# Score products of a head pair as two 64-row products into two banks, and value products of the two halves placed side by side

## The chip, the cores and the metric

The kernel runs on one core of one Trainium2 chip. The metric is the device time of one execution in microseconds (us), as the median of three runs. A core has a matmul engine (TensorE: PE for the products, PEld for the loads of the stationary operand), VectorE (DVE), ScalarE (ACT), GpSimd (POOL) and SyncE (SP), whose queue issues nearly all loads here. Matmul results land in PSUM, which has eight banks of 512 fp32 columns over 128 partitions.

## The reference

Two layers over 256 tokens of width 1024. Layer 0 mixes with a differential attention (4 heads, two score maps each) and an indexed sparse attention (8 query heads on 2 key heads; an indexer of 4 heads of 64 picks 64 keys per query), then a dense feed-forward block. Layer 1 mixes with a block attention (8 heads) and a three-branch attention (8 query heads on 2 key heads: compressed, selected and window keys), then a mixture of 8 experts, of which each token takes 2. With 256 tokens the selected and the window branch and the block attention are all plain causal attention. All heads are 64 wide.

```python
def diff_attention(q, k, v, lam_params, subln_w, lam_init):
    ...
        s = jnp.einsum('bqhjd,bshjd->bhjqs', qb, k, preferred_element_type=F32) * scale
        ...
        p = masked_softmax(s, mask)
        w = p[:, :, 0] - lam * p[:, :, 1]
        return jnp.einsum('bhqs,bshe->bqhe', w.astype(v.dtype), v)
...
def dsa_attention(q, k, v, iq, ik, iw):
    ...
        logits = jnp.einsum('bqhd,bsd->bqhs', iqc, ik, preferred_element_type=F32)
        score = jnp.einsum('bqh,bqhs->bqs', iwc.astype(F32), jax.nn.relu(logits))
        ...
        s = jnp.einsum('bqgrd,bqkgd->bgrqk', qc, kg, preferred_element_type=F32) * scale
        p = masked_softmax(s, ok[:, None, None]).astype(dt)
        return jnp.einsum('bgrqk,bqkgd->bqgrd', p, vg)
...
for l in range(DEPTH):
    x = layer_norm(alpha * x + mixer(x))
    x = layer_norm(alpha * x + (swiglu(x) if l == 0 else moe_swiglu(x)))
```

The last four lines are shortened from the reference's main loop.

## The kernel before, in words

All 256 tokens are two tiles of 128 (NT = 2, index t for rows, qt for queries). Weights are read from HBM as raw tiles of 128x1024 fp32 (load_raw, L115, issued on SP's queue in program order), split into a rounded part wh (ScalarE, L142) and a rest wl (VectorE, L144), and multiplied in three products per block (mm3, L152). The number of raw tiles is fixed; a load waits in SP's queue until the tile that it overwrites has been read. The order of the instructions on each engine is planned by the framework from a simulated timeline, so a function's work may be mixed with that of others; on each engine the planned order is then fixed, and an instruction that waits holds up those behind it. Allocation order in a pool decides which buffer a tile gets.

The attention part works on pairs of heads. Queries are held transposed, 128 partitions for a pair: rows 0 to 63 are one head, 64 to 127 the other (to_heads, L321: transposes into one bank, one copy out). Keys are held the same way but in blocks (to_blocks, L328; blocks_tile, L337): for a pair there are two copies of the width, in the first of which rows 64 to 127 are zero, in the second rows 0 to 63. The zeros are written once by GpSimd (L339, L340), and to_blocks copies the two halves of rows out of PSUM with one instruction each. One product of 128 rows with a moving operand of 2 x nk columns then gives the scores of both heads side by side in one bank.

softmax8 (L346) does this for the eight heads of one query tile with nk = 128 keys (qt = 0) or 256 keys (qt = 1). It goes through groups that fill one bank: two pairs of heads (qt = 0) or one pair (qt = 1). For each group it takes a bank "sps", writes the mask into it with a bf16 product (L356), adds the score products (L359), takes the row maxima with one VectorE instruction (L361) and makes the exponentials on ScalarE, one instruction per head (L364). The banks "sps" come from a ring of two (tag "sp", shared with "hps" of to_heads and a few others). It is called five times for each query tile: diff_probs (keys akB), dsa_probs (bkB), twice in nsa_start (ksB, kwB) and in moba (ckB). The indexer (L455 to L464) makes its scores in the same manner with ikB, two products per query tile, and one Relu per bank (L464).

pv_T (L373) makes the value products transposed: for each key block and each half (first or second head of the pairs) it transposes four blocks of probabilities into a bank "ptps" (L379), copies them out (evac, which alternates between ScalarE and VectorE), and multiplies: with shared values (L385) one product of 512 columns whose result has 64 rows; otherwise (moba, L388) four products of 128 columns. The two halves write the rows 0 to 63 and 64 to 127 of one bank oT.

After the attention come the output projection (mixer_out, L272), a layer norm and, in layer 1, the router and then the experts (L1231), whose weights come in 672 loads of 512 KB.

Of the kernel before, what the change touches and what calls it, by code (L numbers as in the profile page):

```python
# [8 lines left out]
F32 = mybir.dt.float32  # L9
# [4 lines left out]
AF = mybir.ActivationFunctionType  # L14
# [3 lines left out]
P = 128  # L18
# [21 lines left out]
def hybrid_kernel(ctx, tc, x, ev_w_in, ev_w_out, dif_lambda, dif_subln, ffd_w_gate, ffd_w_up, ffd_w_down,  # L40
# [287 lines left out]
    def to_blocks(dst, srcs, t):  # L328

        ps = bank((P, 4, P), "hps")  # L330
        for i, s in enumerate(srcs):
            nc.tensor.transpose(ps[:, i], s, ident)
        for half in range(2):
            r = slice(half * 64, half * 64 + 64)
            evac(dst[r, :, half, t * P:(t + 1) * P], ps[r, :len(srcs)])

    def blocks_tile(pool, n, name):  # L337
        b = pool.tile([P, n, 2, S], F32, name=name)
        nc.gpsimd.memset(b[0:64, :, 1], 0.0)  # L339
        nc.gpsimd.memset(b[64:128, :, 0], 0.0)  # L340
        return b
# [4 lines left out]
    def softmax8(pool, qT, kb_, kslot, qt, maskb, sums):  # L346


        nk = (qt + 1) * P
        ns = 512 // (2 * nk)  # L350
        nm = pool.tile([P, 8], F32, tag="nm", name="nm", bufs=3)
        e = [pool.tile([P, 4, S], F32, tag="e", name="e", bufs=NE_) for _ in range(2)]
        mk = maskb.shape[-1]
        for s0 in range(0, 4, ns):
            ps = bank((P, 2 * ns, nk), "sps")
            nc.tensor.matmul(ps[:, :, nk - mk:], identb, maskb[:, None, :].to_broadcast([P, 2 * ns, mk]),  # L356
                             start=True, stop=False, skip_group_check=True)
            for j in range(ns):
                nc.tensor.matmul(ps[:, 2 * j:2 * j + 2], qT[:, s0 + j, qt * P:(qt + 1) * P],  # L359
                                 kb_[:, kslot(s0 + j), :, :nk], start=False, stop=j == ns - 1, skip_group_check=True)  # L360
            nc.vector.tensor_reduce(nm[:, 2 * s0:2 * (s0 + ns)], ps, axis=AX.X, op=ALU.max, negate=True)  # L361
            for j in range(2 * ns):
                i = 2 * s0 + j
                nc.scalar.activation(e[i // 4][:, i % 4, :nk], ps[:, j], AF.Exp, bias=nm[:, i:i + 1],  # L364
                                     accum_out=sums[:, i:i + 1])
        return e
# [6 lines left out]
    def pv_T(pool, oT, e, qt, vsl, shared, first=True, last=True):  # L373

        for kb in range(qt + 1):
            for half in range(2):
                ps = bank((P, 4, P), "ptps")
                for s_ in range(4):
                    nc.tensor.transpose(ps[:, s_], e[s_ // 2][:, s_ % 2 * 2 + half, kb * P:(kb + 1) * P], ident)  # L379
                pT = pool.tile([P, 4, P], F32, tag="pT", name="pT", bufs=3)  # L380
                evac(pT, ps)
                o = oT[half * 64:half * 64 + 64]
                end = last and kb == qt
                if shared:
                    nc.tensor.matmul(o, vsl(half, kb), pT, start=first and kb == 0, stop=end, skip_group_check=True)  # L385
                else:
                    for s_ in range(4):
                        nc.tensor.matmul(o[:, s_], vsl(2 * s_ + half, kb), pT[:, s_],  # L388
                                         start=first and kb == 0 and s_ == 0, stop=end, skip_group_check=True)
# [29 lines left out]
    bkB = blocks_tile(ap, 1, "bkB")  # L419
    bv = ap.tile([P, NT, P], F32, name="bv")  # L420
    iqT = ap.tile([P, 2, S], F32, name="iqT")
    ikB = blocks_tile(ap, 1, "ikB")
# [3 lines left out]
    akB = blocks_tile(ap, 4, "akB")  # L426
# [3 lines left out]
    def c_b(t, ps):  # L430
        r = roped()
        rope(ap, ps[:, 0:128], 2, t, r[:, 0:128])
        rope(ap, ps[:, 256:512], 4, t, r[:, 256:512])
        nc.scalar.copy(bv[:, t], ps[:, 128:256])
        to_blocks(bkB, [r[:, 0:128]], t)
        to_heads(iqT, [r[:, 256:384], r[:, 384:512]], t)

    def c_i(t, ps):
        r = roped()
        rope(ap, ps[:, 0:64], 1, t, r[:, 0:64])  # L440
        nc.vector.tensor_copy(r[:, 64:128], r[:, 0:64])
        nc.vector.tensor_copy(iw[:, t], ps[:, 64:68])
        to_blocks(ikB, [r[:, 0:128]], t)
# [11 lines left out]
    for qt in range(NT):  # L455
        nk = (qt + 1) * P
        rl = ap.tile([P, 4, S], F32, tag="e", name="rl", bufs=NE_)
        ns = 512 // (2 * nk)
        for s0 in range(0, 2, ns):
            ps = bank((P, 2 * ns, nk), "ips")  # L460
            for j in range(ns):
                nc.tensor.matmul(ps[:, 2 * j:2 * j + 2], iqT[:, s0 + j, qt * P:(qt + 1) * P], ikB[:, 0, :, :nk],
                                 start=True, stop=True)
            nc.scalar.activation(rl[:, 2 * s0:2 * (s0 + ns), :nk], ps, AF.Relu)  # L464
        sc = ap.tile([P, S], F32, tag="score", name="score", bufs=2)
        nc.vector.tensor_scalar(sc[:, :nk], rl[:, 0, :nk], iw[:, qt, 0:1], None, op0=ALU.mult)
        for h in range(1, 4):
            nc.vector.scalar_tensor_tensor(sc[:, :nk], rl[:, h, :nk], iw[:, qt, h:h + 1], sc[:, :nk],
                                           op0=ALU.mult, op1=ALU.add)
        nc.vector.tensor_tensor(sc[:, nk - P:nk], sc[:, nk - P:nk], causalb, ALU.add)  # L470
        m8 = ap.tile([P, 8], F32, tag="m8", name="m8", bufs=2)
        for _ in range(TOPK // 8):
            nc.vector.max(m8, sc[:, :nk])
            nc.vector.match_replace(sc[:, :nk], m8, sc[:, :nk], GONE)
        sb = ap.tile([P, nk], BF16, name=f"selb{qt}")
        nc.vector.tensor_scalar(sb, sc[:, :nk], -2e38, NEG, op0=ALU.is_gt, op1=ALU.mult)
        nc.vector.tensor_tensor(sb[:, nk - P:], sb[:, nk - P:], causalb, ALU.min)
        selb[qt] = sb

    def dsa_probs(qt):  # L480
        return weighted(ap, bqT, bkB, lambda s: 0, qt, selb[qt])
# [6 lines left out]
    def diff_probs(qt):  # L488
        nk = (qt + 1) * P
        sums = ap.tile([P, 8], F32, tag="sums", name="sums", bufs=3)  # L490
        e = softmax8(ap, aqT, akB, lambda s: s, qt, causalb, sums)
# [40 lines left out]
    project(xp, w0[:, 512:1024], 512, c_rope(to_blocks, akB, False))  # L532
# [97 lines left out]
    ksB = blocks_tile(ap, 1, "ksB")  # L630
    kwB = blocks_tile(ap, 1, "kwB")
# [3 lines left out]
    ckB = blocks_tile(lp, 4, "ckB")  # L635
# [17 lines left out]
    def c_kv(t, ps):  # L653
        nc.scalar.copy(kvc[:, t], ps[:, 0:256])
        nc.scalar.copy(vsw[:, t, 0], ps[:, 384:512])
        r = roped()
        rope(ap, ps[:, 256:384], 2, t, r[:, 0:128])
        to_blocks(ksB, [r[:, 0:128]], t)

    def c_w(t, ps):  # L660
# [3 lines left out]
        to_blocks(kwB, [r[:, 0:128]], t)  # L664
# [135 lines left out]
    def nsa_start(qt):  # L800
        oT = mbank("oT", "mo").rearrange("p (s q) -> p s q", q=P)
        for i, kb_ in ((0, ksB), (1, kwB)):
# [16 lines left out]
    def moba(qt):  # L819
        e = weighted(lp, cqT, ckB, lambda s: s, qt, causalb)  # L820
# [84 lines left out]
    project(xp, w1[:, 512:1024], 512, c_rope(to_blocks, ckB, False))  # L905
# [388 lines left out]
```

## Time and profile before

| | us |
|---|---|
| median of 3 runs | 1399.73 (1396.94 to 1402.06) |
| profiled execution | 1404.08 |
| its span, first to last instruction | 1402.2 |
| TensorE busy in the span | 1313.6 (94%) |
| VectorE busy | 753.4 (54%) |
| ScalarE busy | 544.3 (39%) |
| mean granted TensorE clock | 0.967 |

The span has two parts. Up to about 520 us the DMA engines are busy for parts of the time; from there to the end they are busy throughout, at some 400 GB/s. Layer 0's attention lies between about 20 and 122 us, its feed-forward block up to about 310, layer 1's projections and attention between about 310 and 490, the router up to 520.

How to read the rows further below. A row of the stretches has the stretch, its length, then the busy time of PE, PEld, DVE, ACT and POOL (instructions in brackets), the granted clock as a share of 2.4 GHz, the DMA engines' busy share and GB/s. A row of the timeline has the start, the length, the engine, the line and the operation with what it writes and reads, the tile of the array (contraction rows * output rows), the moving operand's shape and how many instructions were merged into the row; in square brackets how long the engine was idle before and what ended it. An fp32 product stands there as two instructions. The length of a matmul includes its way through the array; in a stream the next one starts earlier. A row of a tile or line has the count, then the shortest, median and longest duration in ns, the first and last start, and the shapes.

### The profile page before, as it was taken

To read this page: it belongs to the slowest core of one execution; us is meant where nothing else is said; L and a number is where in the kernel's file an instruction comes from. 1 tells how busy PE (TensorE), PEld (TensorE's weight loads), DVE (VectorE), ACT (ScalarE), POOL (GpSimd) and SP (SyncE) were. 2 spreads that over 40 slices of the span, in tenths; PEclk is the share of its full clock that TensorE was granted. 3 is DMA by queue.
4 is the path that set the end of the run, shared out by engine and by line. 5 is a ranking of instruction groups with operands and counts; after the bars stand their busy time and mean duration, and the time that the engine had idled before them with its cause. 6 is when DMAs were issued, how large, how long until landed. Compare 5 with 4: busy or idle time off the path is not lost. (4 is left out here: it accounts for less than half of the span.)

```text
span 1402.2 us, 18209 instructions
## 1 busy us (share of the span) xinstructions
PE 1313.6 (94%) x6136; PEld 848.1 (60%) x6136; DVE 753.4 (54%) x1194; ACT 544.3 (39%) x796; POOL 48.9 (3%) x79
## 2 busy tenths in 40 slices
PE   8979999998988989999999999999999999999983
PEld 7856888886864753367873356885446886433221
DVE  5977654548577551178863156794227894301004
ACT  4464453533436311066652055673125673100000
POOL 2200000001220000000000000000000000000000
PEclk9999999999999979999999998999999999999996
DMA  9244645535453459999999999998999999999993
GB/s 352 70 135 145 216 162 198 184 118 191 148 151 120 156 200 404 402 409 409 402 397 398 402 409 409 402 383 343 408 402 409 408 402 377 409 402 409 409 402 114
DMA packets 146805, 429.98 MB, mean 307 GB/s; under 512 B 15696, under 2 KB 23280, under 8 KB 146704
## 3 DMA queue, kind: packets, MB, share of 16 engines
q1 hardware_dynamic: 146000, 426.48, 80.2%
q0 software_dynamic: 704, 2.26, 0.5%
q8 instruction: 50, 0.82, 0.2%
q14 instruction: 51, 0.42, 0.1%
HBM read 427.64 MB, written 1.05 MB: 306 GB/s over the span
## 5 line engine op out<-in xcount | busy, mean ns | idle before, releaser
L144 DVE TENSOR_TENSOR wl<-raw,wh 128x1024 fp32r<-128x1024 f32 x378 | 455.3, 1224 | 120.3 <-ACT wh L142 117.2
L142 ACT CAST wh<-raw 128x1024 fp32r<-128x1024 f32 x378 | 389.5, 1047 | 230.0 <-PE pg L158 58.4
L1115 PE MATMUL pgu<-raw,xs 128*64 128x512 f32 x1120 | 266.0, 607 | 3.9 <-DMA raw<-in_moe_w_up_dram 3.1
L1115 PEld LDWEIGHTS pgu<-raw,xs 128*64 128x64 f32 x1120 | 81.6, 139 | 164.5 <-issue 132.2
L1160 PE MATMUL y<-raw,hT_s 128*64 128x512 f32 x560 | 130.8, 598 | 7.2 <-DMA raw<-in_moe_w_down_dram 5.5
L1123 DVE TENSOR_TENSOR h_s<-h_s,pgu 64x512 f32<-64x512 f32 x35 | 24.1, 689 | 190.0 <-ACT h_s L1122 190.0
L1160 PEld LDWEIGHTS y<-raw,hT_s 128*64 128x64 f32 x560 | 37.5, 136 | 93.9 <-issue 62.3
L1122 ACT ACTIVATE h_s<-pgu 64x512 f32<-64x512 f32 x35 | 20.7, 591 | 180.2 <-PE pgu L1115 180.2
L156 PE MATMUL mmps<-wh,xTh 128*128 128x512 f32 (+2 forms) x192 | 76.5, 399 | 1.2 <-ACT wh L142 1.0
L158 PE MATMUL mmps<-wh,xTl 128*128 128x512 f32 (+2 forms) x192 | 75.6, 395 | 1.8 <-DVE xTl L165 1.7
L157 PE MATMUL mmps<-wl,xTh 128*128 128x512 f32 (+2 forms) x192 | 74.3, 389 | 0.5 <-DVE wl L144 0.5
L157 PE MATMUL pg<-wl,xeh 128*128 128x512 f32 x168 | 71.1, 423 | 3.8 <-DVE wl L144 3.8
L156 PE MATMUL pg<-wh,xeh 128*128 128x512 f32 x168 | 72.0, 429 | 1.7 <-ACT wh L142 1.3
L158 PE MATMUL pg<-wh,xel 128*128 128x512 f32 x168 | 70.3, 418 | 0.0
L157 PE MATMUL y<-wl,hTh 128*128 128x512 f32 x168 | 66.7, 397 | 1.2 <-DVE wl L144 1.0
L156 PE MATMUL y<-wh,hTh 128*128 128x512 f32 x168 | 66.6, 396 | 0.8 <-ACT wh L142 0.8
L158 PE MATMUL pu<-wh,xel 128*128 128x512 f32 x168 | 66.8, 397 | 0.0
L157 PE MATMUL pu<-wl,xeh 128*128 128x512 f32 x168 | 66.6, 397 | 0.0
L158 PE MATMUL y<-wh,hTl 128*128 128x512 f32 x168 | 66.2, 394 | 0.0
L156 PE MATMUL pu<-wh,xeh 128*128 128x512 f32 x168 | 65.4, 389 | 0.0
L317 ACT COPY hT_s<-tps 128x256 f32<-128x256 f32 x18 | 6.7, 372 | 135.9 <-PE tps L1142 135.9
L319 DVE COPY hT_s<-tps 128x256 f32<-128x256 f32 x17 | 7.2, 425 | 96.9 <-PE tps L1142 96.9
(376 smaller groups left out, 1918.6 us busy)
## 6 DMA issues: line engine op xcount, KB each, us to landing
raw<-in_moe_w_up_dram SPq DMA_DIRECT2D x224, 512.0 KB, 10.1
raw<-in_moe_w_gate_dram SPq DMA_DIRECT2D x224, 512.0 KB, 10.1
raw<-in_moe_w_down_dram SPq DMA_DIRECT2D x224, 512.0 KB, 10.1
raw<-in_ffd_w_gate_dram SPq DMA_DIRECT2D x22, 512.0 KB, 5.1
raw<-in_ffd_w_up_dram SPq DMA_DIRECT2D x22, 512.0 KB, 4.5
raw<-in_ffd_w_down_dram SPq DMA_DIRECT2D x22, 512.0 KB, 4.7
raw<-in_ev_w_in_dram SPq DMA_DIRECT2D x20, 512.0 KB, 9.0
raw<-in_od_w_in_dram SPq DMA_DIRECT2D x20, 512.0 KB, 4.1
```

The costliest lines, as they stand in the source:

```text
L142: nc.scalar.copy(wh[:, :w], rv)
L144: nc.vector.tensor_tensor(wl[:, :w], rv, wh[:, :w].bitcast(F32), ALU.subtract)
L156: nc.tensor.matmul(ps, ah, wh, start=first and i == 0, stop=False)
L157: nc.tensor.matmul(ps, ah, wl, start=False, stop=False)
L158: nc.tensor.matmul(ps, al, wh, start=False, stop=last and i == n - 1)
L317: nc.scalar.copy(dst, src)
L319: nc.vector.tensor_copy(dst, src)
L1115: nc.tensor.matmul(p_[i * SMALL:(i + 1) * SMALL], xs[:, k0 + k], halves(w[k], n)[j], start=k0 + k == 0, stop=k0 + k == KD - 1)
L1122: nc.scalar.activation(h[:SMALL], p_[:SMALL], AF.Silu)
L1123: nc.vector.tensor_tensor(h[:SMALL], h[:SMALL], p_[SMALL:], ALU.mult)
L1160: nc.tensor.matmul(ys[0][i * SMALL:(i + 1) * SMALL], ts[k], w[:, i * 512:(i + 1) * 512], start=c0 == 0 and k == 0, stop=c0 + n == F_EXP an ...
```

## The change

The keys lose their blocks of zeros: a tile of keys is half as wide, is filled by to_heads as the queries are, and nothing is set to zero. Each score product of a pair becomes two products of 64 contraction rows, one from rows 0 to 63 of queries and keys into one bank, the other from rows 64 to 127 into a second bank. A group of softmax8 now covers two banks at once: all four pairs (qt = 0) or two pairs (qt = 1), with one mask product and one maximum per bank, so the number of mask products, maxima and exponentials stays as it was; the exponentials alternate between the two banks. The indexer does the same, with one Relu per bank written to every second head. In pv_T both halves are transposed and copied out first, and then their products follow each other: the two halves of the shared product, or, in moba, the halves in turn for each of the four pairs.

```diff
-    def to_blocks(dst, srcs, t):
-        ps = bank((P, 4, P), "hps")
-        for i, s in enumerate(srcs):
-            nc.tensor.transpose(ps[:, i], s, ident)
-        for half in range(2):
-            r = slice(half * 64, half * 64 + 64)
-            evac(dst[r, :, half, t * P:(t + 1) * P], ps[r, :len(srcs)])
-
-    def blocks_tile(pool, n, name):
-        b = pool.tile([P, n, 2, S], F32, name=name)
-        nc.gpsimd.memset(b[0:64, :, 1], 0.0)
-        nc.gpsimd.memset(b[64:128, :, 0], 0.0)
-        return b
+    def keys_tile(pool, n, name):
+        return pool.tile([P, n, S], F32, name=name)
+
+    HALVES = (slice(0, 64), slice(64, P))
...
         nk = (qt + 1) * P
-        ns = 512 // (2 * nk)
+        ns = 512 // nk
         nm = pool.tile([P, 8], F32, tag="nm", name="nm", bufs=3)
+        nv = nm.rearrange("p (s h) -> p h s", h=2)
...
         for s0 in range(0, 4, ns):
-            ps = bank((P, 2 * ns, nk), "sps")
-            nc.tensor.matmul(ps[:, :, nk - mk:], identb, maskb[:, None, :].to_broadcast([P, 2 * ns, mk]),
-                             start=True, stop=False, skip_group_check=True)
+            pss = [bank((P, ns, nk), "sps") for _ in HALVES]
+            for ps in pss:
+                nc.tensor.matmul(ps[:, :, nk - mk:], identb, maskb[:, None, :].to_broadcast([P, ns, mk]),
+                                 start=True, stop=False, skip_group_check=True)
             for j in range(ns):
-                nc.tensor.matmul(ps[:, 2 * j:2 * j + 2], qT[:, s0 + j, qt * P:(qt + 1) * P],
-                                 kb_[:, kslot(s0 + j), :, :nk], start=False, stop=j == ns - 1, skip_group_check=True)
-            nc.vector.tensor_reduce(nm[:, 2 * s0:2 * (s0 + ns)], ps, axis=AX.X, op=ALU.max, negate=True)
-            for j in range(2 * ns):
-                i = 2 * s0 + j
-                nc.scalar.activation(e[i // 4][:, i % 4, :nk], ps[:, j], AF.Exp, bias=nm[:, i:i + 1],
-                                     accum_out=sums[:, i:i + 1])
+                for ps, rows in zip(pss, HALVES):
+                    nc.tensor.matmul(ps[:, j], qT[rows, s0 + j, qt * P:(qt + 1) * P], kb_[rows, kslot(s0 + j), :nk],
+                                     start=False, stop=j == ns - 1, skip_group_check=True)
+            for h, ps in enumerate(pss):
+                nc.vector.tensor_reduce(nv[:, h, s0:s0 + ns], ps, axis=AX.X, op=ALU.max, negate=True)
+            for j in range(ns):
+                for h, ps in enumerate(pss):
+                    i = 2 * (s0 + j) + h
+                    nc.scalar.activation(e[i // 4][:, i % 4, :nk], ps[:, j], AF.Exp, bias=nm[:, i:i + 1],
+                                         accum_out=sums[:, i:i + 1])
...
     def pv_T(pool, oT, e, qt, vsl, shared, first=True, last=True):
         for kb in range(qt + 1):
+            pTs = []
             for half in range(2):
...
-                pT = pool.tile([P, 4, P], F32, tag="pT", name="pT", bufs=3)
-                evac(pT, ps)
-                o = oT[half * 64:half * 64 + 64]
-                end = last and kb == qt
-                if shared:
-                    nc.tensor.matmul(o, vsl(half, kb), pT, start=first and kb == 0, stop=end, skip_group_check=True)
-                else:
-                    for s_ in range(4):
-                        nc.tensor.matmul(o[:, s_], vsl(2 * s_ + half, kb), pT[:, s_],
-                                         start=first and kb == 0 and s_ == 0, stop=end, skip_group_check=True)
+                pTs.append(pool.tile([P, 4, P], F32, tag="pT", name="pT", bufs=3))
+                evac(pTs[-1], ps)
+            end = last and kb == qt
+            for s_ in [slice(0, 4)] if shared else range(4):
+                for half, pT in enumerate(pTs):
+                    o = oT[half * 64:half * 64 + 64]
+                    nc.tensor.matmul(o if shared else o[:, s_], vsl(half if shared else 2 * s_ + half, kb), pT[:, s_],
+                                     start=first and kb == 0 and s_ in (0, slice(0, 4)), stop=end,
+                                     skip_group_check=True)
...
-        ns = 512 // (2 * nk)
-        for s0 in range(0, 2, ns):
-            ps = bank((P, 2 * ns, nk), "ips")
-            for j in range(ns):
-                nc.tensor.matmul(ps[:, 2 * j:2 * j + 2], iqT[:, s0 + j, qt * P:(qt + 1) * P], ikB[:, 0, :, :nk],
-                                 start=True, stop=True)
-            nc.scalar.activation(rl[:, 2 * s0:2 * (s0 + ns), :nk], ps, AF.Relu)
+        rv = rl.rearrange("p (s h) k -> p h s k", h=2)
+        pss = [bank((P, 2, nk), "ips") for _ in HALVES]
+        for j in range(2):
+            for ps, rows in zip(pss, HALVES):
+                nc.tensor.matmul(ps[:, j], iqT[rows, j, qt * P:(qt + 1) * P], ikT[rows, 0, :nk], start=True, stop=True)
+        for h, ps in enumerate(pss):
+            nc.scalar.activation(rv[:, h, :, :nk], ps, AF.Relu)
```

The six key tiles bkB, ikB, akB, ksB, kwB and ckB become bkT, ikT, akT, ksT, kwT and ckT, made by keys_tile, and every call of to_blocks becomes one of to_heads.

## Rows read from the trace of the kernel before

**Rows 1.** Stretches: length, busy PE, PEld, DVE, ACT, POOL, clock, DMA, GB/s.

```profile
37.00:64.00 27.00, 27.00 (x122) 21.61 (x122) 25.91 (x63) 11.91 (x15) 5.92 (x8) 1.00 0.25 79
64.00:78.00 14.00, 14.00 (x65) 10.98 (x64) 13.90 (x35) 6.82 (x19) 3.84 (x4) 1.00 0.21 63
78.00:95.00 17.00, 10.53 (x49) 7.15 (x48) 12.51 (x20) 13.43 (x37) 0.00 (x0) 0.95 0.65 192
95.00:104.00 9.00, 8.22 (x35) 5.02 (x34) 6.78 (x25) 3.64 (x13) 0.00 (x0) 0.71 0.22 68
104.00:122.00 18.00, 15.05 (x72) 8.91 (x71) 14.47 (x47) 11.75 (x40) 0.00 (x0) 1.00 0.40 115
...
405.00:450.00 45.00, 40.51 (x192) 26.01 (x191) 39.11 (x89) 28.51 (x84) 6.89 (x5) 1.00 0.35 106
450.00:490.00 40.00, 39.73 (x239) 27.66 (x238) 21.84 (x55) 14.20 (x46) 0.00 (x0) 1.00 0.34 129
...
520.00:1386.00 866.00, 830.12 (x3714) 470.40 (x3710) 399.81 (x439) 320.83 (x377) 0.00 (x0) 0.97 1.00 393
```

**Rows 2.** SP's queue around the experts' start: two issues (timeline) and a wait.

```profile
499.87 0.42 SPq L123 DMA_DIRECT2D raw<-in_moe_w_gate_dram  x1
520.13 0.34 SPq L123 DMA_DIRECT2D raw<-in_moe_w_up_dram  x1
...
SPq L1198 <- DVE countr L964: 14.6, 1, 14.6
```

**Rows 3.** Score products of moba: line L359 by tile, and two timeline rows.

```profile
L359 PE MATMUL sps<-ckB,cqT x16: 379/486/595, 450.2 to 465.2; 128*128 128x256 f32 x8, 128*128 128x512 f32 x8
...
450.23 1.03 PE L359 MATMUL sps<-ckB,cqT 128*128 128x256 f32 x4
...
455.46 1.02 PE L359 MATMUL sps<-ckB,cqT 128*128 128x512 f32 x2
```

**Rows 4.** Shared value products in the timeline, and the first load behind them.

```profile
112.96 1.07 PE L385 MATMUL oT<-pT,bv 128*64 128x512 f32 x2
...
456.85 1.08 PE L385 MATMUL oT<-pT,vsw 128*64 128x512 f32 x4
457.86 0.42 PEld L379 LDWEIGHTS ptps<-ident,e 128*128 128x128 f32 x4 [0.81 <-issue]
...
461.76 1.07 PE L385 MATMUL oT<-pT,vsw 128*64 128x512 f32 x2
...
462.76 0.20 PEld L810 LDWEIGHTS pcT<-ident,ec 128*128 128x128 f32 x2 [0.81 <-issue]
```

**Rows 5.** Products of 128 columns, halves in turn (L815) and not (L388), timeline.

```profile
463.13 1.09 PE L815 MATMUL oT<-pc,vblk 128*64 128x128 f32 x16
464.15 0.42 PEld L379 LDWEIGHTS ptps<-ident,e 128*128 128x128 f32 x4 [0.17 <-issue]
...
485.07 1.58 PE L388 MATMUL oT<-pT,cv 128*64 128x128 f32 x16
...
486.58 1.86 PEld L867 LDWEIGHTS lg<-gwr,zT 128*128 128x128 f32 x16 [0.17 <-issue]
```

**Rows 6.** A wait of 400 to 490 us, the maxima, two exponentials in the timeline.

```profile
PE sps L356 <- ACT e L364: 3.4, 3, 1.4
...
L361 DVE TENSOR_REDUCE nm<-sps x30: 672/683/692, 70.6 to 466.1; 128x2 f32<-128x512 f32 x20, 128x4 f32<-128x512 f32 x10
...
440.94 0.47 ACT L364 ACTIVATE e<-sps,nm 128x256 f32<-128x256 f32 x1 [0.97 <-DVE nm L361]
...
441.40 0.47 ACT L364 ACTIVATE e<-sps,nm 128x256 f32<-128x256 f32 x1
```

**Rows 7.** Copies of a half of the keys by VectorE, by tile.

```profile
L319 DVE COPY akB<-hps x2: 694/694/695, 49.6 to 55.9; 64x512 f32<-64x512 f32 x2
```

**Rows 8.** Score products after TensorE's pause in layer 0, timeline.

```profile
96.29 1.91 PE L359 MATMUL sps<-bkB,bqT 128*128 128x512 f32 x2
```

**Rows 9.** Products of 64 contraction rows, by line.

```profile
L1182 PE MATMUL cps<-yh,dT x32: 386/492/789, 631.0 to 1381.4; 64*128 64x512 f32 x20, 128*128 128x512 f32 x12
```

More of the change, by code (lines that the diff above doesn't have):

```diff
@@ L417, in hybrid_kernel @@
     NE_ = 4
-    bkB = blocks_tile(ap, 1, "bkB")
+    bkT = keys_tile(ap, 1, "bkT")
     bv = ap.tile([P, NT, P], F32, name="bv")
     iqT = ap.tile([P, 2, S], F32, name="iqT")
-    ikB = blocks_tile(ap, 1, "ikB")
+    ikT = keys_tile(ap, 1, "ikT")
     iw = ap.tile([P, NT, 4], F32, name="iw")
@@ L425, in hybrid_kernel @@
     aqT = ap.tile([P, 4, S], F32, name="aqT")
-    akB = blocks_tile(ap, 4, "akB")
+    akT = keys_tile(ap, 4, "akT")
     av = ap.tile([P, NT, 512], F32, name="av")
@@ L434, in c_b @@
         nc.scalar.copy(bv[:, t], ps[:, 128:256])
-        to_blocks(bkB, [r[:, 0:128]], t)
+        to_heads(bkT, [r[:, 0:128]], t)
         to_heads(iqT, [r[:, 256:384], r[:, 384:512]], t)
@@ L442, in c_i @@
         nc.vector.tensor_copy(iw[:, t], ps[:, 64:68])
-        to_blocks(ikB, [r[:, 0:128]], t)
+        to_heads(ikT, [r[:, 0:128]], t)
     def c_rope(to, dst, scaled, gqa=False):
@@ L480, in dsa_probs @@
     def dsa_probs(qt):
-        return weighted(ap, bqT, bkB, lambda s: 0, qt, selb[qt])
+        return weighted(ap, bqT, bkT, lambda s: 0, qt, selb[qt])
     def dsa_out(qt, e):
@@ L490, in diff_probs @@
         sums = ap.tile([P, 8], F32, tag="sums", name="sums", bufs=3)
-        e = softmax8(ap, aqT, akB, lambda s: s, qt, causalb, sums)
+        e = softmax8(ap, aqT, akT, lambda s: s, qt, causalb, sums)
         rs = ap.tile([P, 8], F32, tag="rs", name="rs", bufs=3)
@@ L531, in hybrid_kernel @@
     x1 = act.tile([P, NT, D], F32, tag="res", name="x1", bufs=2)
-    project(xp, w0[:, 512:1024], 512, c_rope(to_blocks, akB, False))
+    project(xp, w0[:, 512:1024], 512, c_rope(to_heads, akT, False))
     project(xp, w0[:, 0:512], 512, c_rope(to_heads, aqT, True))
@@ L629, in hybrid_kernel @@
     cv = lp.tile([P, NT, 512], F32, name="cv")
-    ksB = blocks_tile(ap, 1, "ksB")
-    kwB = blocks_tile(ap, 1, "kwB")
+    ksT = keys_tile(ap, 1, "ksT")
+    kwT = keys_tile(ap, 1, "kwT")
     kvc = ap.tile([P, NT, S], F32, name="kvc")
@@ L634, in hybrid_kernel @@
     gate = ap.tile([P, NT, 24], F32, name="gate")
-    ckB = blocks_tile(lp, 4, "ckB")
+    ckT = keys_tile(lp, 4, "ckT")
     gateb = ap.tile([P, 24], F32, name="gateb")
@@ L657, in c_kv @@
         rope(ap, ps[:, 256:384], 2, t, r[:, 0:128])
-        to_blocks(ksB, [r[:, 0:128]], t)
+        to_heads(ksT, [r[:, 0:128]], t)
     def c_w(t, ps):
@@ L663, in c_w @@
         rope(ap, ps[:, 0:128], 2, t, r[:, 0:128])
-        to_blocks(kwB, [r[:, 0:128]], t)
+        to_heads(kwT, [r[:, 0:128]], t)
         g = gate[:, t]
@@ L801, in nsa_start @@
         oT = mbank("oT", "mo").rearrange("p (s q) -> p s q", q=P)
-        for i, kb_ in ((0, ksB), (1, kwB)):
+        for i, kb_ in ((0, ksT), (1, kwT)):
             e = weighted(lp, drT, kb_, lambda s: 0, qt, causalb, gates(qt, 1 + i))
@@ L819, in moba @@
     def moba(qt):
-        e = weighted(lp, cqT, ckB, lambda s: s, qt, causalb)
+        e = weighted(lp, cqT, ckT, lambda s: s, qt, causalb)
         oT = mbank("oT", "mo").rearrange("p (s q) -> p s q", q=P)
@@ L904, in hybrid_kernel @@
     ec = compressed()
-    project(xp, w1[:, 512:1024], 512, c_rope(to_blocks, ckB, False))
+    project(xp, w1[:, 512:1024], 512, c_rope(to_heads, ckT, False))
     os_ = [nsa_start(qt) for qt in range(NT)]
```

## The prediction

> **What bounds the kernel now.** I read the stretches first [rows 1]. From 520 to 1386 us the DMA engines are busy 1.00 of the time at 393 GB/s: the experts' weights set the pace there. The question is what sets the start. SP's queue shows it [rows 2]: it issues its last early expert load at 499.87 us and the next one at 520.13; in between it waits 14.6 us for the router's counts (L1198) and then for tiles that the first expert products free. Some 20 us without an issue mean that loads are not what the experts' start waits for. So a microsecond by which layer 1's attention ends earlier is a microsecond off the end, and one lost there is lost at the end. The change touches only the attention, so its worth is read from the stretches before 490 us, one by one.
>
> There the bound changes [rows 1]. From 450 to 490 us it is TensorE: 39.73 of 40.00 us busy, VectorE 21.84. From 405 to 450 it is TensorE (40.51 of 45) with VectorE hardly less busy (39.11). From 37 to 78 both are full, VectorE 25.91 of 27 and 13.90 of 14 with the choice of the indexed keys. From 78 to 95 no engine is full (TensorE 10.53 of 17). From 95 to 122 TensorE has 23.27 of 27 and VectorE 21.25.
>
> **Score products.** The tile's line lists 16 instructions for moba's eight products, 8 of 256 and 8 of 512 columns [rows 3]. Four of 256 columns take 1.03 us together and one alone 0.379, so the starts are (1.03 - 0.379)/3 = 0.217 us apart; for 512 columns it is 1.02 - 0.595 = 0.425. One set of scores (both query tiles) costs 8 x 0.217 + 8 x 0.425 = 5.1 us of TensorE. There are five such sets, 25.7 us, and the indexer with half as many products of the same shapes, 2.6 us.
>
> After the change each product is two, of half the columns and half the rows. If the two run beside each other, half the time goes: 12.8 + 1.3 = 14.1 us. If they run one after the other, the number of columns passed is the same and nothing goes. No row has two row halves in turn: the only 64-row products are those of the experts' results, which use one half of the rows at a time [rows 9]. The nearest rows are column halves. Two single products of one half take 1.00 us until the next load starts (461.76 to 462.76), and four instructions, both halves, take 1.01 (456.85 to 457.86) [rows 4]: there the second half is free. In small products the same is seen: 16 instructions with the halves in turn take 1.02 us (463.13 to 464.15), without the turn 1.51 (485.07 to 486.58) [rows 5]. I take the overlap also for the row halves, since the array is divided in the same way, and keep zero as the other end.
>
> The Trainium skill, "TensorEngine Tiling (Array Packing)", section Key Properties, says that different tiles of the array can load and multiply in parallel, and by its table of theoretical speedups two tiles are worth up to 2x; by that estimate the 14.1 us would go whole. It also says that a change of the tiling mode empties the array first.
>
> What leaving and re-entering the full array costs is in the rows: 1.00 us for two products that stream 2 x 0.425 = 0.85, so 0.15 us a time. A set of scores now has three groups of 64-row products (one for qt = 0, two for qt = 1) and the indexer two: 17 x 0.15 = 2.6 us. Net per set: 2.57 - 0.45 = 2.1 us, five sets 10.6; the indexer 1.3 - 0.3 = 1.0.
>
> **Value products.** L385 has 36 instructions, 18 products. Four times both halves already stand together (456.85 is one); the other ten are single, the first at 112.96, the last at 461.76 [rows 4]. Five pairs formed of these save 5 x (2 x 1.00 - 1.01) = 5.0 us. In moba the three groups of 16 go from 1.51 to 1.02 us [rows 5]: 1.5 us. What it asks: both transposes and both copies come before the first product. Three buffers for the copies remain, so a third copy can go ahead while two are read.
>
> **Copies and zeros.** Each to_blocks made two copies of 64 rows where to_heads makes one of 128 at the length of one. VectorE loses one of its two copies of akB, 0.69 us [rows 7], in the stretch where it is full. The others lie beside a busy TensorE and count nothing; uncovered, twelve tiles' second copies would be worth at most 12 x 0.69 = 8 us. The zeros go from GpSimd, which is busy 5.92 of 27 us or less [rows 1] and which nobody waits for here: nothing.
>
> **The sum by stretches.** TensorE's own saving is 10.6 + 1.0 + 5.0 + 1.5 = 18.1 us. How much passes through:
> - 450 to 490: one set 2.1, two pairs 2.0, moba 1.5, together 5.6. TensorE is full and VectorE has 18 us to spare: all of it passes.
> - 405 to 450: two sets 4.2, two pairs 2.0, together 6.2. VectorE's 39.11 us stay. If VectorE were as full at the end as TensorE is now (40.51/45 = 0.90), the stretch would be 39.11/0.90 = 43.4 us long: 1.6 us pass. Bounds 0 and 6.2.
> - 95 to 122: one set 2.1 and one pair 1.0. TensorE has 3.7 us of pauses and is waited for at the rest: I take half, 1.5. Bounds 0 and 3.1.
> - 37 to 95: the indexer 1.0 and one set 2.1, but VectorE is the bound and then no engine is: only VectorE's copy counts, 0.7. Bounds 0 and 3.1 + 0.7.
>
> Together 5.6 + 1.6 + 1.5 + 0.7 = 9.4 us. The profiled execution took 1404.08 us (span 1402.2 and 1.9 around it), so it would be 1394.7. It lies 4.35 above the median of the runs, 1399.73, from which the forecast is 1399.73 - 9.4 = **1390.3 us**.
>
> **Rivals.**
> 1. The row halves do not overlap. Then a set costs 0.45 us more instead of 2.1 less. 450 to 490 gives 2.0 + 1.5 - 0.45 = 3.1, 95 to 122 half of 1.0 - 0.45 = 0.3, the copy 0.7, 405 to 450 nearly nothing: 4.1 us, **1395.6**. For it: no row shows row halves. Against it: both kinds of column halves do overlap.
> 2. Slower: TensorE waits for ScalarE because a group holds both banks. Before, groups of qt = 1 took the two banks of the ring by turns, and TensorE waited for exponentials 3.4 us in all in layer 1 [rows 6]. Now the second group of a set needs both banks back: two maxima of 0.68 and four exponentials at 0.46 (440.94 to 441.40), 1.4 + 1.8 = 3.2 us, once in each of five sets, 16 us. Less the 3.4 it is 12.6 us more, if TensorE's queue has nothing else to place there. Behind the waiting mask product stand transposes and projections, and for those wait the copies and the weight splits. Then only 450 to 490 and the copy would keep their gain: 12.6 - 5.6 - 0.7 = +6.3, **1406**. It decides when more than 9.4 us, three of the five waits, are uncovered. For it: TensorE already waits for exponentials with two turns [rows 6]. Against it: elsewhere projections or the output products fill, and the planner orders the work anew. The Trainium skill, same page, section Gotcha 1: PSUM Pressure, warns that row tiles need different banks and so press on PSUM; the wait here is what it would look like.
> 3. The clock. After TensorE's pauses before 95 us it was granted 0.71 from 95 to 104 [rows 1], and two products of 512 columns took 1.91 us there [rows 8] against 1.02. That stretch lost 9.0 x 0.29 = 2.6 us. With 6.2 us less to do, TensorE pauses more from 405 to 450, where the clock is 1.00 now. Two such falls cost 5.2 us: 9.4 - 5.2 = 4.2, **1395.5**. The Trainium skill, "TensorE: Matmul & The Clock Gate", section Why this matters for your kernels, has the rule that pauses between bursts of products bring the half clock back; the row at 95 us agrees.
> 4. All of it passes: VectorE's and ScalarE's work moves into the gaps, 18.1 + 0.7 = 18.8 us, **1381**.
>
> **How the numbers follow.** Forecast 0.54 (own range 1385 to 1395), rival 1 0.15, rival 2 0.13, rival 3 0.08, rival 4 0.10. About 0.3%, 4.2 us, is what a measurement of this kernel can tell from no change: faster means below 1395.5, slower above 1403.9. Faster: 0.50 of the forecast's 0.54, all of rival 4 and a little under half of rivals 1 and 3, the whole 0.67. Slower: most of rival 2, with 0.02 for an order that turns out worse: 0.13. The same: 0.20. The range goes from rival 4's 1381 to 1403, just short of rival 2, and leaves out about 0.18.
>
> **What the profile after would show.** Right: L359 with tiles 64*128, 32 instructions a set, and TensorE busy for scores at half; a group's starts at half of 0.217 and 0.425 us apart; L385 only in rows of four; moba's groups of 16 at 1.0 us; the experts' first product some 9 us earlier, and the same length of time from there to the end. Rival 1 shows in starts as far apart as the halved columns alone make them. Rival 2 shows in the wait of mask products (L356) for exponentials: over 9 us in all. Rival 3 shows in a clock under 1.00 from 405 to 450. The forecast would be wrong at its root if the time from the first expert product to the end changed.

## The result: slower, and the profile after

The changed kernel takes 1414.45 us (median; 1410.61 to 1417.14), the kernel before on the same chip 1400.71: a ratio of 1.0092, 95% interval [1.0072, 1.0112]. Timed again later it took 1412.88 against 1401.75, 1.0075 [1.0059, 1.0091]. The forecast was 1390.3 us, with a range from 1381 to 1403.

The profiled execution took 1410.61 us, the fastest of its runs, where the profiled one of before was the slowest of its own (1404.08); so the two traces lie 6.5 us apart, less than the medians (13.7). First the stretches of the changed kernel, with the columns of [rows 1]; its attention ends some 10 us later, so the experts' stretch is moved by 10.

```profile
95.00:104.00 9.00, 8.04 (x35) 5.04 (x36) 7.82 (x29) 3.87 (x18) 0.00 (x0) 0.81 0.36 122
104.00:122.00 18.00, 15.76 (x89) 9.89 (x88) 13.95 (x45) 11.91 (x42) 0.00 (x0) 1.00 0.38 121
405.00:430.00 25.00, 25.00 (x141) 19.64 (x139) 18.05 (x40) 10.29 (x34) 3.42 (x5) 0.93 0.15 43
430.00:450.00 20.00, 18.23 (x75) 10.96 (x74) 16.72 (x34) 14.14 (x37) 0.00 (x0) 0.95 0.58 178
450.00:490.00 40.00, 39.22 (x200) 24.26 (x200) 19.45 (x48) 15.83 (x55) 0.00 (x0) 0.90 0.22 83
530.00:1396.00 866.00, 826.03 (x3716) 466.04 (x3712) 402.88 (x448) 321.09 (x377) 0.00 (x0) 0.98 1.00 393
```

The experts still run at 393 GB/s. TensorE is still full or nearly so from 405 to 490, but at 0.93, 0.95 and 0.90 of its clock, where both stretches of before had 1.00. The timeline of the same kernel shows what became of the two halves of moba's scores, of the value products (L385) and of the key scores of the first query tile (columns: start, us, engine, line, operation, tiles, shape, count).

```profile
413.60 1.16 PE L354 MATMUL sps<-ksT,drT 64*128 64x128 f32 x14
...
460.49 0.38 PE L350 MATMUL sps<-causalb,identb 128*128 128x512 bf16 x1
460.80 1.16 PE L354 MATMUL sps<-ckT,cqT 64*128 64x128 f32 x8
461.89 1.08 PE L385 MATMUL oT<-pT,vsw 128*64 128x512 f32 x4
462.90 0.33 PE L377 MATMUL ptps<-ident,e 128*128 128x128 f32 x1
463.06 0.38 PE L350 MATMUL sps<-causalb,identb 128*128 128x512 bf16 x1
463.37 0.93 PE L354 MATMUL sps<-ckT,cqT 64*128 64x128 f32 x6
...
468.47 1.07 PE L385 MATMUL oT<-pT,vsw 128*64 128x512 f32 x2
...
480.95 1.09 PE L385 MATMUL oT<-pT,cv 128*64 128x128 f32 x14
```

The program issues the halves in turn, but the planned order does not keep them so: half A goes out whole (x8 at 460.80), then other work, then half B with a mask of its own (463.06). I take the reason to be that half A's bank is free before half B's; no run tests that. Where that happened the halves don't overlap: 8 instructions take 1.16 us. At 413.60 they came in turn, and 14 take the same 1.16 us. Row halves do run beside each other, then; 13 of the changed kernel's 15 groups of attention scores are ordered so that they can't.

Where the time went, by the starts of five products in each trace (A: layer 0's first output product; B: first product of the compression of keys, L702 before; C: `kc`, L749 before; D: layer 1's first output product; E: first expert product). Medians belong to each kernel's own chip job; before had 1399.73 to 1401.75 in them.

| kernel | A | A to B | B to C | C to D | D to E | E | median | ratio |
|---|---|---|---|---|---|---|---|---|
| before | 118.8 | 260.8 | 28.0 | 62.6 | 46.2 | 516.4 | 1400.71 | |
| changed | 119.4 | 259.8 | 32.9 | 70.7 | 44.9 | 527.6 | 1414.45 | 1.0092 |
| value part alone | 120.3 | 260.8 | 30.0 | 61.8 | 45.3 | 518.2 | 1401.78 | 1.0011 |
| score part alone | 123.0 | 259.8 | 33.1 | 71.6 | 45.9 | 533.4 | 1415.82 | 1.0116 |
| copies alone | 115.2 | 259.8 | 32.3 | 62.9 | 46.2 | 516.4 | 1402.90 | 1.0005 |
| changed, 128 rows | 117.2 | 259.7 | 33.0 | 63.3 | 45.3 | 518.5 | 1401.52 | 0.9997 |
| changed, last product 64 rows | 121.2 | 260.5 | 31.9 | 67.9 | 45.3 | 526.7 | 1412.48 | 1.0077 |
| in turn | 124.4 | 260.8 | 33.2 | 69.3 | 46.9 | 534.6 | 1418.27 | 1.0119 |
| in turn, 128 rows | 122.6 | 259.8 | 33.4 | 70.9 | 45.2 | 531.8 | 1414.40 | 1.0095 |

From E to the end the profiled executions of all kernels take 880 to 888 us, with no order in it; a single trace says no more than that of the experts.

### The profile page after: what moved, and what is told of

It reads as the page before. It is cut to its first block, busy times and chain, and to the rows that moved or that the text cites. A ratio compares the mean times of both kernels' runs of the same rounds, so it can differ in the third digit from the quotient of the medians.

```text
span 1408.8 us, 18366 instructions
## 1 busy us (share of the span) xinstructions
PE 1326.0 (94%) x6224; PEld 857.4 (61%) x6224; DVE 754.2 (54%) x1188; ACT 542.6 (39%) x791; POOL 40.2 (3%) x67
## 3 DMA queue, kind: packets, MB, share of 16 engines
HBM read 427.64 MB, written 1.05 MB: 304 GB/s over the span
## 5 line engine op out<-in xcount | busy, mean ns | idle before, releaser
L156 PE MATMUL pg<-wh,xeh 128*128 128x512 f32 x168 | 70.9, 422 | 1.7 <-ACT wh L142 1.3
```

The source lines that it names most:

```text
L156: nc.tensor.matmul(ps, ah, wh, start=first and i == 0, stop=False)
```

## The experiments

**Which part.** Before with the change's value products alone (halves transposed and copied first, then the products side by side), and the changed kernel with before's value products (the first in outline):

```
-    for half in range(2): transposes; copy; products
+    for half in range(2): transposes; copy
+    for s_ ...: for half in range(2): product
```

> The kernel before with the value products part alone (both halves' probabilities transposed and copied, then the products of the halves side by side in program order); scores with the blocks of zeros, as before. The change as a whole cost about 13 us (1414.45 against 1400.71). Theory (the loss sits in the scores, whose two halves the planned order kept apart): this kernel is within 4 us of before, 1397 to 1405; the planned order leaves about eight of the ten single 64-row value products single, so next to nothing is saved. Rival (the value part holds three pT buffers until both halves are copied and delays the transposes): 1406 to 1415, and the waits of the copies into pT for products grow. Rival (clock): no row-halved score product runs here, so no clock below 1.00 between 385 and 470 us.

> The changed kernel with the value products of before: the score part alone. Theory (scores kept apart by the planned order): it keeps most of the loss, 1408 to 1416, and half batches stand alone again (x8 of 64x128 in about 1.16 us). Rival (the value part is the cost): 1390 to 1401. Rival (clock): the clock is below 1.00 somewhere between 385 and 470 us, and the end of layer 1's attention is later by about the clock's loss.

Measured: 1.0011 [0.9999, 1.0023] and 1.0116 [1.0091, 1.0140]. The whole loss comes with the score part. The value part saves nothing that can be timed: its trace still has ten single value products of shared values (L388 there), and the 1.5 us saved in moba's groups (4.7 to 3.2 us busy) doesn't show in the time. My clock clause failed: it has 0.87 from 400 to 410 us, with no 64-row scores in it.

**A new plan without new work.** `flip = [0]` to `flip = [1]` in before.

> The kernel before with one change that alters no work: the copies out of PSUM that alternate between ScalarE and VectorE start with the other engine, so each copy changes place and the planned order differs throughout the attention. It sizes what a new plan alone can do. Theory (order of halves) expects within 4 us of before, 1397 to 1405. Rival (any new plan moves the time by about 10 us, so the change's loss is the luck of a plan): more than 7 us from before, to either side.

1402.05, ratio 1.0007 [0.9995, 1.0019], though every copy that alternates changes its engine and TensorE's order shifts with it. This new plan alone is not worth 13 us.

**The halves in turn.** The products of a group are chained on TensorE:

```
+            with products_in_order():   # mask A, mask B, A0, B0, A1, B1, ...
```

> The changed kernel, with the score products of a group (and the indexer's) chained on TensorE: mask A, mask B, then products of half A and B in turn. Nothing else differs. Theory (the order denied the overlap): groups run as x14 to x16 of 64x128 in about 1.2 us and x8 of 64x256 in about 1.0 us, the first expert product comes 5 to 12 us earlier than in the changed kernel (527.6), and the time is 1394 to 1405. Rival (two banks per group, lost alternation with ScalarE): the score work shrinks the same, but the wait of the mask product for the exponentials grows past 9 us and the time stays 1408 to 1418. Rival (clock falls follow from row-halved products): the score work shrinks, yet the clock is half for 10 us or more between 390 and 460 us, and the time stays over 1406.

1418.27, ratio 1.0119 [1.0099, 1.0138]: my theory, that the order alone had denied the gain, fell. The next rows are its timeline from 440 to 455 us (in brackets the idle time ahead and what ended it).

```profile
440.14 1.13 PE L355 MATMUL sps<-ksT,drT 64*128 64x256 f32 x8
441.21 1.09 PE L378 MATMUL ptps<-ident,e 128*128 128x128 f32 x8
445.56 0.27 PE L351 MATMUL sps<-causalb,identb 128*128 128x256 bf16 x1 [3.26 <-ACT e L362]
445.76 1.08 PE L386 MATMUL oT<-pT,vsw 128*64 128x512 f32 x4
449.22 0.37 PE L351 MATMUL sps<-causalb,identb 128*128 128x256 bf16 x1 [2.38 <-ACT e L362]
449.52 2.08 PE L355 MATMUL sps<-ksT,drT 64*128 64x256 f32 x8
453.50 0.37 PE L351 MATMUL sps<-causalb,identb 128*128 128x256 bf16 x1 [1.90 <-ACT e L362]
454.41 0.37 PE L351 MATMUL sps<-causalb,identb 128*128 128x256 bf16 x1 [0.54 <-ACT e L362]
```

The halves now overlap: 8 instructions of 256 columns at full clock in 1.13 us, the time of 4 in the changed kernel. And each group in these rows waits for the one before it to be through ScalarE, since it needs both banks back. After the second wait the clock is at half (granted 0.50 from 449 to 459 us), and the same 8 take 2.08 us. The masks' wait for exponentials from 85 to 530 us (total, count, longest), before, in turn (14.0 of it at the causal mask), in turn with 128 rows, and with 128 rows not in turn (the last two are described below):

```profile
PE sps L356 <- ACT e L364: 5.1, 5, 1.4
```
```profile
PE sps L351 <- ACT e L362: 14.9, 9, 4.2
```
```profile
PE sps L351 <- ACT e L362: 11.8, 8, 4.1
```
```profile
PE sps L350 <- ACT e L361: 5.0, 4, 1.8
```

**128 rows in place of 64, and the copies.** The changed kernel with whole rows in its score products, and before with the change's copies (its products read `kb_[:, slot, None, :nk]` for both halves):

```
-  nc.tensor.matmul(ps[:, j], qT[rows, ...], kb_[rows, kslot(s0 + j), :nk], ...)
+  nc.tensor.matmul(ps[:, j], qT[:, ...], kb_[:, kslot(s0 + j), :nk], ...)
```

> The changed kernel, with one thing altered: its score products (and the indexer's) take all 128 rows of the queries and keys in place of 64, so each half's product sums both heads; the scores are therefore not the reference's. Number, columns, banks and copies are the changed kernel's, and the planned order of layer 1 is nearly so. There is no switch to 64 rows and back, and no work on half the rows. Turn stayed at 1418 with its scores cheaper, so the order alone is not the cause. Theory 1 (work on 64 rows is what costs: switches, and a clock that falls to half in the pauses that the kernel before went through at full clock): 1396 to 1405, clock 1.00 from 440 to 460 us. Theory 2 (two banks to a group, and the plan that comes of it): 1409 to 1419 as the changed kernel, and the last output product of attention ends near 510 us.

> The kernel before with the copies of the change alone: keys copied whole, no blocks of zeros and no memsets; its score products keep 128 rows, one bank and all columns, and read the same keys for both halves, so each score sums both heads and is not the reference's. Theory 1 (64 rows) and theory 2 (two banks) both expect within 4 us of before, 1397 to 1405. Rival 3 (fewer copies shift the plan ahead of the compressed keys: the one pause of 6.0 us before line 727's product, in place of 2.1 and 2.9, and the half clock behind it, which made 4.4 us by 412 us in the changed kernel): the pause of about 6 us is here too, and the time 1403 to 1408.

0.9997 [0.9982, 1.0013] and 1.0005 [0.9993, 1.0017]. With the banks, halves and copies of the change, but whole rows, nothing is lost. The copies alone do have a pause of 5.7 us before the product that follows the copy of cmp_hs (L726 in the kernel before). It is 6.0 us in the changed kernel; before, two pauses of 2.1 and 2.9 us stood there. Behind the one long pause the next eight instructions take 1.88 us, against 1.05 before (the clock is granted at 0.50 from 391.8 to 393.6 us). B to C is 4 to 5 us longer in every kernel with these copies. But they pay: A is 3.6 us earlier, A to B 1.0 us shorter. So this is not the loss, against rival 3 of that expectation. A group of moba in the kernel with whole rows, then one in the changed kernel:

```profile
461.33 0.27 PE L350 MATMUL sps<-causalb,identb 128*128 128x256 bf16 x1
461.44 1.03 PE L354 MATMUL sps<-ckT,cqT 128*128 128x256 f32 x4
462.39 1.07 PE L385 MATMUL oT<-pT,vsw 128*64 128x512 f32 x2
```
```profile
465.62 0.27 PE L350 MATMUL sps<-causalb,identb 128*128 128x256 bf16 x1
465.82 1.13 PE L354 MATMUL sps<-ckT,cqT 64*128 64x256 f32 x4
466.88 1.07 PE L385 MATMUL oT<-pT,vsw 128*64 128x512 f32 x2
```

From mask to next work 1.06 us against 1.26: entering 64 rows costs 0.09 us (0.20 less 0.11), leaving 0.11. There a product of tile 128*64 follows in both kernels. Where 128*128 work follows, it is 0.98 against 1.27: entering costs 0.10 us, leaving 0.19 (whole rows first).

```profile
430.85 0.28 PE L350 MATMUL sps<-causalb,identb 128*128 128x256 bf16 x1
430.97 1.03 PE L354 MATMUL sps<-ksT,drT 128*128 128x256 f32 x4
431.83 1.04 PE L377 MATMUL ptps<-ident,e 128*128 128x128 f32 x8
```
```profile
436.43 0.28 PE L350 MATMUL sps<-causalb,identb 128*128 128x256 bf16 x1
436.65 1.13 PE L354 MATMUL sps<-ksT,drT 64*128 64x256 f32 x4
437.70 1.09 PE L377 MATMUL ptps<-ident,e 128*128 128x128 f32 x8
```

The Trainium skill, "TensorEngine Tiling (Array Packing)", section Key Properties, says that a change of tiling mode drains the engine; these rows agree, with 0.20 and 0.29 us for both passages.

**More banks, and the changed kernel again.**

```
-            pss = [bank((P, ns, nk), "sps") for _ in HALVES]
+            pss = [bank((P, ns, nk), n) for n in ("sps", "spb")]   # spb: the transposes' ring
```

> As the kernel with the products in turn, but half B's bank comes from the two that the transposes use, so that a group's two banks are no longer both of the pair that the scores had: four banks serve scores and transposes together. Theory 2 (two banks to a group end the alternation with the exponentials; the mask product waited 14.0 us for them between 85 and 530 us in the kernel in turn, 4.0 us before): that wait falls below 7 us and the time to 1400 to 1410. Theory 1 (64 rows): the wait may fall, but the time stays over 1410, with the clock at half somewhere between 390 and 470 us.

> The changed kernel once more, for its time on this chip beside the others and for a second trace of it. If the clock's falls belong to the kernel, they come again near 391 to 403, 416 to 421 and 447 to 458 us (each within 3 us); if they are chance, they come elsewhere or not at all. 1410 to 1418.

The four banks made it worse, 1428.58, 1.0194 [1.0174, 1.0214]: the masks still wait 14.0 us (14.9 in turn), and the transposes, whose ring is now shared, wait 5.7 us for the scaled probabilities (0.9 in turn). So it doesn't show what a bank more would be worth. The changed kernel's clock fell at the same places again: 0.80 from 415 to 420 us (0.74 in its first trace), 0.50 from 450 to 455 in both.

**In turn with whole rows; the last product alone on 64; the first query tile alone.** The second has `HALVES if j == ns - 1 else [slice(0, P)] * 2`; the third is before with `if qt == 0:` and the group in turn, on slices `kb_[rows, slot, h, :nk]` of the block keys.

> The kernel in turn with 128 rows in its score products (each score sums both heads, so it is not the reference's): the order in turn and the two banks to a group stay, the work on 64 rows goes. In turn the products cost half and yet the mask product waited 14.0 us for exponentials between 85 and 530 us and the time was 1418. Theory 1 (64 rows alone cost, two banks nothing, as the kernel with full rows says at 1401.5): 1397 to 1405. Theory 2, narrowed (two banks cost only where the order takes both at once): 1406 to 1418, with 10 us or more of that wait. A mixture, which I think likeliest: 1402 to 1409, the wait at 6 to 12 us.

> The changed kernel, but of each half's products in a group only the last takes 64 rows, the others 128 (those sum both heads, so the scores are not the reference's). Every half batch still goes into the 64-row work and out again once, as in the changed kernel, while the work on 64 rows falls to a half of the columns at 256 keys and a quarter at 128. The rows of the changed kernel beside those with full rows give 0.09 to 0.11 us for each passage in or out, 3.6 us for the 18 half batches of layer 1, and some 5 us to the clock. If the passages are the whole cost: 1410 to 1416, as the changed kernel. If the clock is the whole, and follows the amount of work on 64 rows: 1400 to 1406. Both, as I read them: 1404 to 1411, with the passages' 0.2 us per half batch kept and less than 3 us lost to the clock from 405 to 460 us.

> The kernel before, with only the scores of the first 128 queries as two 64-row halves in turn (there a score set fills two banks either way, so no bank is held that was free before); the second 128 queries, the indexer and the value products as before. Four sets have about 1.1 us of 64-row products in place of 2.1 us, and one passage in and out (0.2 us). Theory (64 rows pay for themselves where the halves overlap and no alternation is lost, if the clock holds): 1396 to 1402. Rival (the clock falls after these too): 1402 to 1408, with the clock below 1.00 between 413 and 425 us.

1.0095 [1.0076, 1.0114], 1.0077 [1.0057, 1.0096], 1.0021 [1.0008, 1.0034]. In turn with whole rows is slow without any 64-row work: against whole rows not in turn, C to D grows by 7.6 us (63.3 to 70.9). In that stretch TensorE is idle for 10.5 us in place of 5.3, and its clock is 0.93 in place of 0.97. The masks' wait (11.8 against 5.0 us) says that holding both banks is a cause; the order, which now lets nothing in between the halves, may be another, and no run parts the two. Against it, 64 rows in turn give back only 1.6 us of C to D (70.9 to 69.3). With 64 rows in the last product alone, nearly all of the loss is there, though its planned order in layer 1 is nearly that of whole rows: it doesn't follow the amount of 64-row work. The first tile alone gains nothing. Its group in turn takes 1.16 us, but the clock falls right behind it, with TensorE busy throughout:

```profile
405.00:410.00 5.00, 5.00 (x44) 3.84 (x43) 4.91 (x9) 2.10 (x2) 2.59 (x3) 1.00 0.00 0
410.00:415.00 5.00, 5.00 (x25) 4.16 (x25) 3.36 (x9) 3.71 (x17) 0.00 (x0) 0.72 0.40 108
```

**The passages alone.** In before, behind each of the 30 masks:

```
+            nc.tensor.matmul(ps[:, 0, 0:8], qT[0:64, s0, ...], zcol[0:64], start=False, stop=False, ...)
```

and the same with `0:P`. The two have the same planned order.

> The kernel before, with one product more in each of its 30 groups of scores: 8 columns of zeros over 64 rows, added right behind the mask. It alters no score, and its work is next to nothing, but each group now goes into 64-row work and out again, 30 times in all (18 in layer 1's two branches and moba), as often as the changed kernel's 30 half batches of attention scores do. If passages cost 0.2 us each and nothing else: 1.5 to 2.5 us later by the end of layer 0's attention, 3.6 us in layer 1, 1404 to 1409, clock 1.00 from 405 to 435 us. If passages also bring the clock down: 1407 to 1415, with half clock for 5 us or more between 405 and 460 us. If the amount of 64-row work decides: within 2 us of tiny_128.

> The same products of 8 columns of zeros, over all 128 rows: the planned order is that of tiny_64, instruction by instruction, and no row is left out. It is the measure for tiny_64. 30 products of two instructions of some 0.03 to 0.06 us each, 2 to 4 us, a half of it in layer 1: 1400 to 1405, if a new plan does no more than it did for the copies begun on the other engine (1402.05).

1410.06, 1.0071 [1.0050, 1.0091], and 1404.36, 1.0029 [1.0012, 1.0045]. The same group in both, 64 rows first:

```profile
453.84 0.27 PE L359 MATMUL sps<-causalb,identb 128*128 128x256 bf16 x1
454.04 0.39 PE L361 MATMUL sps<-zcol,drT 64*128 64x8 f32 x2
454.36 1.12 PE L364 MATMUL sps<-kwB,drT 128*128 128x512 f32 x2
455.41 1.07 PE L390 MATMUL oT<-pT,vsw 128*64 128x512 f32 x2
```
```profile
451.94 0.27 PE L359 MATMUL sps<-causalb,identb 128*128 128x256 bf16 x1
452.05 0.29 PE L361 MATMUL sps<-zcol,drT 128*128 128x8 f32 x2
452.19 1.10 PE L364 MATMUL sps<-kwB,drT 128*128 128x512 f32 x2
453.23 1.07 PE L390 MATMUL oT<-pT,vsw 128*64 128x512 f32 x2
```

1.57 us against 1.29: a passage in and out costs 0.28 us here, where 128*128 work follows; 18 of them make 5.0 us in layer 1. C to D is 73.1 against 69.0 us, 4.1 more, A 1.1 later, and the medians differ by 5.7 us. So the passages cost on their own, close to their price in the rows. My clause that they also bring down the clock isn't borne out: from 435 to 455 us the two lose 3.1 and 2.6 us to it. The second has no 64-row scores at all, and before had 1.00 there.

## Why the prediction was wrong

- **What bounds the kernel: held.** The experts' part kept its length within its scatter (880 to 888 us), and what the attention lost came out at the end: E is 11.1 us later.
- **Score products: the step that failed.** "If the two run beside each other, half the time goes" was weighed as a question to the array; the array does it (14 instructions in 1.16 us against 8). It was a question to the planned order. I took the order of the program for that of TensorE, though [rows 4] already showed that the two differ: in the kernel before, the program puts the second half's transposes and copy between the value products of the halves, and yet four pairs stand together. So in 13 of 15 groups no time went, as in rival 1, and its sum for that case (1395.6) was too kind:
- **The passages.** I charged 17 of 0.15 us, one per group, and read the 0.15 from column halves. With the halves apart there is one per half batch, and where other work cuts a half batch in two, one more: the changed kernel's timeline has 21 in layer 1's three sets, 11 in layer 0's two and 4 in the indexer. Five of the 21 have a 128*64 product behind them; at 0.20 us for these and 0.29 for the rest, layer 1 pays by this estimate 5.6 us in place of my 1.4 (nine groups at 0.15).
- **The clock, rival 3,** weighed for 405 to 450 after less work. It fell with the same amount of work, and later as well. By windows, busy time times missing clock, 405 to 490 us: 25.00 x 0.07 + 18.23 x 0.05 + 39.22 x 0.10 = 6.6 us in the changed kernel; with whole rows, by the next two rows, 15.40 x 0.09 = 1.4 (405 to 430 has 1.00 there).

```profile
430.00:450.00 20.00, 15.40 (x72) 10.47 (x70) 15.77 (x27) 14.00 (x40) 0.00 (x0) 0.91 0.64 185
450.00:490.00 40.00, 39.32 (x259) 27.98 (x257) 22.68 (x59) 14.39 (x48) 0.00 (x0) 1.00 0.29 106
```

- **The sum from C to D**, changed against whole rows, is 7.4 us. Passages 5.6 and clock 5.2 make 10.8. The changed kernel pauses 2.7 us less (2.6 against 5.3 us idle), and its one group in turn there gives back 0.6 (14 instructions in 1.16 us, 1.72 with whole rows). That comes to 7.5. The clock is read to two digits over 80 us, so the sum is good to about half a us on either side. Another 2.2 us are lost before A (119.4 against 117.2), where the other 15 passages would be 3.0 at 0.20. Which of the falls are the 64 rows' doing is open, and of whole rows there is one trace: the last-product kernel, with half the 64-row work or less, loses nothing from 410 to 420 us and as much from 450 to 455.
- **Rival 2 was right in its mechanism, at another place.** In the changed kernel it doesn't act: its masks wait 1.5 us for exponentials from 400 to 490 us. It acts as soon as the halves are in turn. I priced a wait at 3.2 us; the trace has 3.26, 2.38, 1.90 and 0.54. So the forecast's gain was barred on both sides: apart, the halves pay passages and clock; in turn, they pay the waits.
- **Value products:** of the 5.0 us at most 1.0 came. The changed kernel has eight single products in place of ten; in the planned order the second half's transposes still come between. Moba's groups do run at 1.0 us, as forecast.
- **Copies:** 0.7 us forecast, 3.6 by A and 1.0 more by B measured alone, and lost again from B to C, in a chain that I had not looked at because the change doesn't touch it.
- **Chances:** the 0.67 for faster holds 0.07 of the 0.23 of rivals 1 and 3, under a third and not "a little under half".

## What to carry to other kernels

Where a planner sets the order, as here, tiles of TensorE that are to run beside each other must be held in turn by explicit order, and then each group holds a bank per tile: count how many groups the ring still holds before counting the columns saved. Passages into 64-row work and out are paid per visit, not per column, so short batches lose by them even where nothing else changes: products of 8 columns cost this kernel 5.7 us more on 64 rows than on 128. A loss can be taken apart when one kernel keeps order, banks and copies and changes the rows alone, and another the order alone.

## What the runs showed of the hardware

- A passage into 64-row work and out cost 0.20 us around a half batch with a 128*64 product behind it, 0.29 us with 128*128 work behind it, and 0.28 us around a product of 8 columns.
- The clock fell with TensorE busy 5.00 of 5.00 us on both sides, behind a group of 64-row products in turn and 16 instructions of 30 columns (L777 of the changed kernel) that follow it: 0.74 and 0.80 from 415 to 420 us in two traces of the changed kernel, 0.72 from 410 to 415 with the first tile alone, 0.66 from 420 to 425 with the score part alone. With whole rows at the same place, behind the same 16 instructions, it was 1.00. But in the kernel in turn it stayed at 1.00 behind the same group, and with the value part alone it was 0.74 from 400 to 405 us, TensorE busy 5.00 of 5.00, with no 64-row scores at all, behind a pause of 3.7 us. That it is the 64 rows is likely, not shown.

The next rows are 415 to 420 us, then 450 to 455, of the changed kernel, and the same with whole rows. The second fall has a shorter fellow with whole rows, some 6 us earlier at the same scores (window keys): 0.91 from 430 to 450 us, shown above.

```profile
415.00:420.00 5.00, 5.00 (x25) 4.21 (x25) 3.44 (x9) 3.67 (x17) 0.00 (x0) 0.74 0.41 108
...
450.00:455.00 5.00, 5.00 (x16) 3.10 (x16) 2.04 (x4) 2.56 (x9) 0.00 (x0) 0.50 0.07 26
```
```profile
415.00:420.00 5.00, 5.00 (x25) 3.97 (x24) 4.93 (x15) 3.25 (x13) 1.61 (x2) 1.00 0.22 49
...
450.00:455.00 5.00, 5.00 (x27) 2.77 (x25) 4.12 (x13) 1.22 (x4) 0.00 (x0) 1.00 0.00 0
```
